# Stick-breaking attention with queries on the partitions: a reversed scan and transposes in place of products with ones

## The chip, the cores and the metric

The kernel runs on one core of a Trainium2 chip. The metric is the device time of one execution in microseconds (us), and the median over the runs is what counts.

## The reference

Three blocks follow one another on 512 tokens of width 2048, all in float32. The first block has an RWKV-7 recurrence, a pooling mixer and a stick-breaking attention; the second has chunked attention beside a state-space model (S5); the third has a forgetting attention. The change lies in the stick-breaking attention (12 heads of 64). Cut to what matters:

```
for q0 in range(0, S, 128):
    z = q[q0:q0+128] @ k[:q0+128].T
    causal = key < query
    log_1m = where(causal, log_sigmoid(-z), 0)
    after = reversed_cumsum(log_1m, over keys) - log_1m
    w = where(causal, exp(log_sigmoid(z) + after), 0)
    out = w @ v[:q0+128]
```

So each weight needs the sum of `log_1m` over all later keys of its row.

## The kernel before

Dense projections dominate. `dense` (line 286) yields after each of 16 k-steps of a unit; a step is three float32r matmuls of 512 columns (lines 310 to 312: high and low halves of weights and activations). Weights come by DMA in tiles of four steps and are split by `split_w` into a high part (`wh`, made by ScalarE, or by GpSimd where `POOL_SPLITS` says so) and a low part (`wl`, always VectorE). The splits run up to three tiles, some twelve steps, ahead of the matmuls that use them.

The order of every compute engine's instructions is the order of the program text. `stick` (line 1766) works on six pairs of heads, j = 0 to 5. While it handles pair j it calls `pump(n)`, which takes n steps out of a stream: the projections of pair j+1 (64 steps), or for the last pair two pooling groups and the first part of the output projection (87 steps). What `pump` has not taken is run at the end of the pair by a bare loop over the stream. The numbers of steps stand in `STICK_STEPS`; here they add up to 57 in each pair. `pump` also advances a side job, `extra`, once for every 1/`EXTRA_RATE` steps, which is every second step in `stick`; the bare loop does not. The side job is `s5_params` (line 899): 58 advances of small VectorE arithmetic for the S5 layer, and then eight tables, each of 14 advances on GpSimd and one DMA pair (lines 1004 to 1019). Whatever is left of it is emitted by `finish(self.extra)` after `stick`, ahead of the output projection `out_proj`. There, `s5_prep` computes with GpSimd and VectorE in turns, beginning in the third unit.

One pair before the change, with keys on the partitions (E and N are 128 x 1280 tiles holding four triangular key blocks):

- for each of the two heads: `scores` into three PSUM banks named `sm`; ScalarE takes Abs, Exp, Ln; pumped steps; VectorE makes E (log-sigmoid of z) and N (its counterpart, line 1811) and masks N; ScalarE and VectorE split N into `sbh` and `sbo`; in the first head the products with the values of the previous pair (`values`, line 1777) come next; pumped steps
- for each head: 20 matmuls of `sbh` and `sbo` with a triangle and with ones (line 1832) into three `sm` banks; VectorE subtracts them from E; ScalarE takes Exp; pumped steps; VectorE masks E; pumped steps.

There are four `sm` banks in all. A bank comes free when its last reader is done.

Of the kernel before, what the change touches and what calls it, by code (L numbers as in the profile page):

```python
# [9 lines left out]
F32 = mybir.dt.float32  # L10
F32R = mybir.dt.float32r
# [3 lines left out]
OP = mybir.AluOpType  # L15
# [15 lines left out]
STICK_WAIT = (8,6)  # L31
HEAD_LAG = (3,5,7)
RWKV_STEPS = (0,0,0,(13,6),4,4,3,3,3,1,1)
STICK_STEPS = ((7,7),(9,7),(4,8),(4,11))
EVEN_STEPS = ((3,8),(6,8),10)
ODD_STEPS = ((4,20),16)
LAST_STEPS = ((4,16),14)
# [103 lines left out]
class Kern:  # L141
# [49 lines left out]
    def constants(self, tmp):  # L191
        nc, c = self.nc, self.const
        jp = tmp.tile([128, 128], I32, name="jp")
        nc.gpsimd.iota(jp, pattern=[[1, 128]], base=0, channel_multiplier=-1)
        mk = lambda name: c.tile([128, 128], F32, name=name)
        self.ident = mk("ident")
        nc.vector.tensor_scalar(self.ident, jp, 0.0, None, op0=OP.is_equal)

        self.m16 = c.tile([128, 2], F32, name="m16")
        nc.vector.tensor_reduce(self.m16, self.ident.rearrange("p (a e i) -> p e a i", e=2, i=16),  # L200
                                op=OP.add, axis=mybir.AxisListType.XY)

        self.id2 = c.tile([128, 64], F32, name="id2")
        self.add(self.id2, self.ident[:, 0:64], self.ident[:, 64:128])

        self.m_lt = mk("m_lt")
        nc.vector.tensor_scalar(self.m_lt, jp, 0.0, None, op0=OP.is_gt)

        self.mk2 = c.tile([128, 2, 64], F32, name="mk2")
        for h in (0, 1):  # L210
            r = slice(64 * h, 64 * h + 64)
            nc.vector.tensor_scalar(self.mk2[r, 0], jp[r, r], 0.0, None, op0=OP.is_ge)
            nc.vector.tensor_scalar(self.mk2[r, 1], jp[r, r], 0.0, -1.0 if h == 0 else 1.0, op0=OP.is_gt, op1=OP.mult)

        blk = tmp.tile([128, 128], F32, name="blk")
        nc.vector.memset(blk, 0.0)
        for h in (0, 1):
            nc.vector.memset(blk[64 * h:64 * h + 64, 64 * h:64 * h + 64], 1.0)
        mr = lambda name: c.tile([128, 128], F32R, name=name)
        self.blk_r = mr("blk_r")  # L220
        self.copy(self.blk_r, blk)
        self.cen_r = mr("cen_r")
        V = nc.vector
        V.scalar_tensor_tensor(self.cen_r, blk, -1.0 / 64, self.ident, op0=OP.mult, op1=OP.add)
        self.heads = c.tile([128, 2], F32, name="heads")
        V.tensor_copy(self.heads, blk[:, 0:128:64])
        self.ident_r = mr("ident_r")
        self.copy(self.ident_r, self.ident)
        self.one = c.tile([128, 1], F32, name="one")
        nc.vector.memset(self.one, 1.0)  # L230
        self.ones_r = mr("ones_r")
        self.copy(self.ones_r, self.one.to_broadcast([128, 128]))

        self.suf_r = c.tile([128, 128], F32R, name="suf_r")
        nc.vector.tensor_scalar(self.suf_r, jp, 0.0, None, op0=OP.is_lt)

        self.omu = c.tile([128, 25], F32, name="omu")
        o, w = _PV["mu_a"]
        nc.vector.tensor_scalar(self.omu, self.pvt[:, o:o + w], -1.0, 1.0, op0=OP.mult, op1=OP.add)
        o, w = _PV["k_a"]  # L240
        self.oka = c.tile([128, 6], F32, name="oka")
        nc.vector.tensor_scalar(self.oka, self.pvt[:, o:o + w], -0.5, 1.0, op0=OP.mult, op1=OP.add)
        self.half = {}
        for n in ("k_a", "a0", "w0", "b_glu_2"):
            o, w = _PV[n]
            self.half[n] = c.tile([128, w], F32, name="half_" + n)
            nc.vector.tensor_scalar(self.half[n], self.pvt[:, o:o + w], 0.5, None, op0=OP.mult)
        self.qg8 = c.tile([128, 1], F32, name="qg8")
        nc.vector.tensor_scalar(self.qg8, self.pv("qn_g"), 0.125, None, op0=OP.mult)

        self.ipos = c.tile([128, 16], F32, name="ipos")
        nc.gpsimd.iota(self.ipos, pattern=[[1, 16]], base=1, channel_multiplier=0,
                       allow_small_or_imprecise_dtypes=True)
        nc.vector.reciprocal(self.ipos, self.ipos)

        self.reset = c.tile([128, 8, 64], BF16, name="reset")
        nc.vector.memset(self.reset, 1.0)
        nc.vector.memset(self.reset[:, :, 0:1], 0.0)
# [1500 lines left out]

    def causal(self, t):  # L1760

        d = t.rearrange("p (b n) -> p b n", n=256)[:, 0::2, 0:128]
        self.mul(d, d, self.m_lt[:, None, :].to_broadcast([128, 3, 128]))
        self.mul(t[:, 896:1024], t[:, 896:1024], self.m_lt)

    def stick(self, pool, tm, yd, acts, rs, yl):
        nc = self.nc
# [14 lines left out]

        last = None
        self.second_parts(pool)
        for j in range(6):
            pools = self.pools(6 + j, pool, tm, yd, acts, rs)
            self.stream = chain(self.stick_front(tm, j + 1, acts, rs, pool), *pools) if j < 5 else chain(
                *pools, self.out_ahead("w_out", *self.out_operands(yl, yd)))
            q, k, vt, gate = self.ready.pop(j)
            if j == 0:  # L1790
                q, k = self.stacked_q(pool, q), self.stacked_k(pool, k)
                self.pump(FIRST_STEPS)
            sums = []
            self.where = 2 if j else 1
            for p in (0, 1):
                z = [self.small() for _ in range(3)]
                at = lambda b: (z[OFF[b] // 512], OFF[b] % 512)
                for b in (0, 1, 3, 2):
                    t, o = at(b)
                    self.scores(t[:, o:o + 512 - 128 * b], p, slice(128 * b, 512), slice(128 * b, 128 * b + 128), q, k,  # L1800
                                True)
                N = L = pool.tile([128, 1280], F32, name="sbl", bufs=1)
                E = pool.tile([128, 1280], F32, name="sbe", bufs=3)
                for (o, n), t in zip(BANK, z):
                    self.act(L[:, o:o + n], t[:, 0:n], AF.Abs)
                self.act(L, L, AF.Exp, scale=-1.0)
                self.act(L, L, AF.Ln, bias=1.0)
                self.pump(STICK_STEPS[p][0])
                for (o, n), t in zip(BANK, z):
                    V.scalar_tensor_tensor(E[:, o:o + n], t[:, 0:n], 0.0, L[:, o:o + n], op0=OP.min, op1=OP.subtract)  # L1810
                    V.scalar_tensor_tensor(N[:, o:o + n], t[:, 0:n], 0.0, L[:, o:o + n], op0=OP.max,
                                           op1=OP.add)
                self.causal(N)
                hi = pool.tile([128, 1280], F32R, name="sbh", bufs=2)
                lo = pool.tile([128, 1280], F32R, name="sbo", bufs=2)
                self.split(hi, lo, N)
                sums.append((E, hi, lo))
                if last and p == 0:
                    values(*last)
                self.pump(STICK_STEPS[p][1])  # L1820
            for p, (E, hi, lo) in enumerate(sums):
                s = [self.small() for _ in range(3)]
                for b in (0, 1, 3, 2):
                    t, o = s[OFF[b] // 512], OFF[b] % 512
                    mm = []
                    for b2 in range(b, 4):
                        n = 512 - 128 * b2
                        for x in (hi, lo):
                            mm.append((t[:, o + 128 * (b2 - b):o + 128 * (b2 - b) + n],
                                       self.suf_r if b2 == b else self.ones_r, x[:, OFF[b2]:OFF[b2] + n]))  # L1830
                    for i, (o_, l_, r_) in enumerate(mm):
                        nc.tensor.matmul(o_, l_, r_, start=(i == 0), stop=(i == len(mm) - 1))
                for (o, n), t in zip(BANK, s):
                    self.sub(E[:, o:o + n], E[:, o:o + n], t[:, 0:n])
                self.act(E, E, AF.Exp)
                self.pump(STICK_STEPS[2 + p][0])
                self.causal(E)
                self.pump(STICK_STEPS[2 + p][1])
            last = j, vt, [E for E, _, _ in sums], gate
            self.where = 3  # L1840
            if j == 5:
                self.where = 0
                values(*last)
                self.out_last(gate, "w_out")
            for _ in self.stream:
                pass
# [74 lines left out]
```

## Time and profile before

| what | value |
|---|---|
| median of three runs | 3025.04 us (3021.55 to 3025.7) |
| profiled execution, time / span | 3014.29 us / 3012.5 us |
| TensorE matmul busy | 2935.8 us, 97% of the span |
| VectorE, ScalarE, GpSimd busy | 54%, 38%, 17% |
| mean granted TensorE clock | 0.987 of full speed |
| stick-breaking stage | about 598 us to 943 us of the span |

PE is TensorE, DVE is VectorE, ACT is ScalarE, POOL is GpSimd. Times in the views are us from the start of the span.

### The profile page before, as it was taken

What the parts mean: (1) busy time and instruction counts of PE and PEld (TensorE: products, weight loads), DVE (VectorE), ACT (ScalarE), POOL (GpSimd) and SP (SyncE); (2) the same over time, 40 slices, a digit from 0 to 9 for tenths busy, and PEclk for the clock granted to TensorE, in tenths of its full rate; (3) what the DMA queues carried; (4) which work ended last, traced back from release to release, by engine and by line L of the source; (5) the groups of instructions that cost most, each with busy time, mean ns of one, the idle gap of its engine ahead of it and who ended that gap; (6) DMA issues with size and microseconds to landing.
All of it is one profiled execution on the core that took longest, in us unless ns stands there. A gap on an engine that the chain in (4) does not pass through costs nothing. (4 is left out here: it accounts for less than half of the span.)

```text
span 3012.5 us, 42942 instructions
## 1 busy us (share of the span) xinstructions
PE 2935.8 (97%) x16068; PEld 2400.4 (80%) x16068; DVE 1618.0 (54%) x3140; ACT 1134.9 (38%) x2043; POOL 498.8 (17%) x951
## 2 busy tenths in 40 slices
PE   7999999999999999999999999999999999999998
PEld 5777777878887777788888887878888888888887
DVE  7555555477667665655554456344444444444533
ACT  4444443354454223222344454233333232323432
POOL 4111111014764220211100000111101010100011
PEclk9999999999999999999999999999999999999999
DMA  4212122322235556455433325443333333323443
GB/s 141 64 59 60 55 60 69 95 75 84 90 95 167 155 163 196 133 158 157 138 105 103 104 85 177 147 130 109 101 105 96 98 96 97 95 92 95 147 122 119
DMA packets 195298, 334.03 MB, mean 111 GB/s; under 512 B 29696, under 2 KB 44672, under 8 KB 193936
## 3 DMA queue, kind: packets, MB, share of 16 engines
q1 hardware_dynamic: 193808, 327.08, 35.9%
q0 software_dynamic: 1280, 4.20, 0.4%
q8 instruction: 126, 2.06, 0.3%
q14 instruction: 84, 0.69, 0.1%
HBM read 289.55 MB, written 42.70 MB: 110 GB/s over the span
## 5 line engine op out<-in xcount | busy, mean ns | idle before, releaser
L310 PE MATMUL big<-hi,wh 128*128 128x512 f32 x3440 | 1375.7, 400 | 4.1 <-ACT hi L180 2.9
L312 PE MATMUL big<-hi,wl 128*128 128x512 f32 x3440 | 1350.9, 393 | 7.3 <-DVE wl L162 6.8
L311 PE MATMUL big<-lo,wh 128*128 128x512 f32 x3440 | 1349.1, 392 | 2.3 <-DVE lo L162 2.3
L162 DVE TENSOR_TENSOR wl<-wr,wh 128x512 fp32r<-128x512 f32 x884 | 648.3, 745 | 721.0 <-ACT wh L180 711.7
L312 PEld LDWEIGHTS big<-hi,wl 128*128 128x128 f32 x3440 | 649.6, 189 | 153.5 <-DVE wl L162 15.8
L310 PEld LDWEIGHTS big<-hi,wh 128*128 128x128 f32 x3440 | 649.7, 189 | 150.0 <-issue 10.7
L311 PEld LDWEIGHTS big<-lo,wh 128*128 128x128 f32 x3440 | 650.1, 189 | 133.2 <-DVE lo L162 5.6
L180 ACT ACTIVATE wh<-wr 128x512 fp32r<-128x512 f32 x820 | 505.8, 626 | 632.0 <-PE big L311 515.7
L1231 POOL TENSOR_SCALAR dm<-cb,cq 128x128 f32<-128x128 f32 (+1 forms) x64 | 42.4, 663 | 598.1 <-DVE mx L674 580.1
L680 ACT ACTIVATE pm<-pm,mx 128x128 f32<-128x128 f32 (+3 forms) x128 | 70.5, 552 | 178.1 <-DVE mx L676 178.1
L162 POOL TENSOR_TENSOR ssq<-ssq,sq 128x512 f32<-128x512 f32 (+1 forms) x43 | 54.6, 1269 | 380.1 <-ACT sq L175 359.5
L162 DVE TENSOR_TENSOR tm<-big,rs 128x512 f32<-128x512 f32 x86 | 59.2, 688 | 73.4 <-PE big L312 73.3
L175 ACT ACTIVATE sq<-xn 128x512 f32<-128x512 f32 (+1 forms) x47 | 28.8, 613 | 177.8 <-DVE xn L162 166.3
L279 POOL CAST wh<-wr 128x512 fp32r<-128x512 f32 x64 | 47.7, 747 | 143.5 <-PE big L311 93.0
L180 ACT ACTIVATE pt<-sm 128x512 f32<-128x512 f32 (+3 forms) x96 | 43.4, 526 | 62.7 <-PE sm L708 62.7
L162 DVE TENSOR_TENSOR xn<-big,xr 128x512 f32<-128x512 f32 (+1 forms) x50 | 33.3, 667 | 56.7 <-PE big L312 45.5
L1610 POOL MEMSET xi<- 64x16 f32 x6 | 0.7, 119 | 371.4 <-DVE xi L1609 371.4
L180 ACT ACTIVATE qk<-tm 128x512 fp32r<-128x512 f32 x32 | 20.2, 633 | 96.2 <-DVE tm L1366 48.1
L162 POOL TENSOR_TENSOR ssq<-xn 128x512 f32<-128x512 f32 x3 | 3.1, 1040 | 310.4 <-DMA wr<-w_out_even 143.5
L162 DVE TENSOR_TENSOR pl<-sm,pt 128x512 fp32r<-128x512 f32 (+1 forms) x48 | 25.9, 596 | 44.3 <-ACT pt L180 44.3
L686 DVE TENSOR_SCALAR pm<-pm,sm 128x128 f32<-128x128 f32 (+3 forms) x128 | 43.3, 400 | 1.1
L1366 DVE SCALAR_TENSOR_TENSOR tm<-big,rs 128x512 f32<-128x512 f32 x34 | 23.4, 689 | 36.9 <-PE big L312 36.9
(445 smaller groups left out, 3140.4 us busy)
## 6 DMA issues: line engine op xcount, KB each, us to landing
wr<-w_in_odd SPq DMA_DIRECT2D x256, 256.0 KB, 3.3
wr<-w_in SPq DMA_DIRECT2D x228, 256.0 KB, 3.1
wr<-w_in_even SPq DMA_DIRECT2D x192, 256.0 KB, 3.5
wr<-w_out SPq DMA_DIRECT2D x64, 256.0 KB, 3.8
wr<-w_out_even SPq DMA_DIRECT2D x64, 256.0 KB, 3.4
wr<-w_out_odd SPq DMA_DIRECT2D x64, 256.0 KB, 3.3
xr<-x SPq DMA_DIRECT2D x48, 256.0 KB, 3.0
yl<-y SPq DMA_DIRECT2D x45, 256.0 KB, 3.8
```

The costliest lines, as they stand in the source:

```text
L162: (eng or self.nc.vector).tensor_tensor(out, a, b, op=op)
L175: self.nc.scalar.activation(out, x, f, scale=scale)
L180: self.nc.scalar.activation(out, x, AF.Copy, scale=scale)
L279: self.nc.gpsimd.tensor_copy(wh, wr)
L310: nc.tensor.matmul(ps, wh[:, i], hi, start=(k == 0), stop=False)
L311: nc.tensor.matmul(ps, wh[:, i], lo, start=False, stop=False)
L312: nc.tensor.matmul(ps, wl[:, i], hi, start=False, stop=(k == n - 1))
L680: nc.scalar.activation(d, d, AF.Exp, bias=mx[:, b:b + 1], accum_out=sm[:, b:b + 1])
L686: V.tensor_scalar(d, d, sm[:, b:b + 1], None, op0=OP.mult)
L1231: nc.gpsimd.tensor_scalar(D[:, QOFF[b]:QOFF[b] + n], cb[:, 0:n], -1.0, cq[:, b, h:h + 1], op0=OP.mult, op1=OP.add)
L1366: self.nc.vector.scalar_tensor_tensor(t, ps, scale, rs, op0=OP.mult, op1=OP.mult)
L1610: G.memset(X.rearrange("p i c -> p (i c)")[:, 0:256:17], 1.0)
```

## The change

Queries go on the partitions and keys along the free axis, in the layout that `qblocks` and `turn` already use in the second block. The 20 matmuls with triangle and ones and the split of N go. In their place one `tensor_tensor_scan` per head runs backwards over the 1280 columns (`rows` holds a 0 where a block of keys begins anew), and one subtraction in SBUF takes the sums, shifted by a column, from E. The finished weights are turned by `keys(p)`, that is `turn`: ten float32 transposes into three `sm` banks and three ScalarE copies to SBUF, since `values` needs the keys on the partitions. The order within a pair changes: the scan, subtraction and Exp of the first head now come ahead of the second head's scores; the first head is masked and turned inside the second head's part, the second one at the end. `STICK_STEPS` changes with it and adds up to 37 in each pair. `EXTRA_RATE` stays.

```
-STICK_STEPS = ((7,7),(9,7),(4,8),(4,11))
+STICK_STEPS = ((7,0,5,3),(6,2,4,7),3)
...
-        self.ones_r = mr("ones_r")
-        self.copy(self.ones_r, self.one.to_broadcast([128, 128]))
...
+        self.m_gt = mk("m_gt")
+        nc.vector.tensor_scalar(self.m_gt, jp, 0.0, None, op0=OP.is_lt)
...
     def causal(self, t):
-        d = t.rearrange("p (b n) -> p b n", n=256)[:, 0::2, 0:128]
-        self.mul(d, d, self.m_lt[:, None, :].to_broadcast([128, 3, 128]))
-        self.mul(t[:, 896:1024], t[:, 896:1024], self.m_lt)
+        m = self.m_gt[:, None, :].to_broadcast([128, 2, 128])
+        d = t[:, 384:640].rearrange("p (b n) -> p b n", n=128)
+        self.mul(d, d, m)
+        d = t[:, 768:1280].rearrange("p (b n) -> p b n", n=256)[:, :, 128:256]
+        self.mul(d, d, m)
...
+        self.rows = pool.tile([128, 1280], BF16, name="rows", bufs=1)
+        V.memset(self.rows, 1.0)
+        for b in range(4):
+            o = 1279 - (QOFF[b] + 128 * b + 127)
+            V.memset(self.rows[:, o:o + 1], 0.0)
...
+            def keys(p):
+                W.append(pool.tile([128, 1280], F32, name="sbw", bufs=3))
+                self.turn(Es[p], W[p])
...
             for p in (0, 1):
-                z = [self.small() for _ in range(3)]
...
+                z = self.qblocks()
+                for b in (3, 0, 2, 1):
+                    t, o, n = z[b]
+                    self.scores(t[:, o:o + n], p, slice(128 * b, 128 * b + 128), slice(0, n), q, k, False)
+                z = [z[3][0], z[0][0], z[1][0]]
...
                 self.pump(STICK_STEPS[p][0])
+                if p:
+                    self.causal(Es[0])
                 for (o, n), t in zip(BANK, z):
                     V.scalar_tensor_tensor(E[:, o:o + n], t[:, 0:n], 0.0, L[:, o:o + n], op0=OP.min, op1=OP.subtract)
                     V.scalar_tensor_tensor(N[:, o:o + n], t[:, 0:n], 0.0, L[:, o:o + n], op0=OP.max,
                                            op1=OP.add)
                 self.causal(N)
-                hi = pool.tile([128, 1280], F32R, name="sbh", bufs=2)
-                lo = pool.tile([128, 1280], F32R, name="sbo", bufs=2)
-                self.split(hi, lo, N)
-                sums.append((E, hi, lo))
-                if last and p == 0:
+                if p:
+                    self.pump(STICK_STEPS[p][1])
+                    keys(0)
+                elif last:
                     values(*last)
-                self.pump(STICK_STEPS[p][1])
-            for p, (E, hi, lo) in enumerate(sums):
-                s = [self.small() for _ in range(3)]
...
-                        nc.tensor.matmul(o_, l_, r_, start=(i == 0), stop=(i == len(mm) - 1))
-                for (o, n), t in zip(BANK, s):
-                    self.sub(E[:, o:o + n], E[:, o:o + n], t[:, 0:n])
+                self.pump(STICK_STEPS[p][2])
+                V.tensor_tensor_scan(N[:, ::-1], self.rows, N[:, ::-1], 0.0, OP.mult, OP.add)
+                self.sub(E[:, 0:1279], E[:, 0:1279], N[:, 1:1280])
                 self.act(E, E, AF.Exp)
-                self.pump(STICK_STEPS[2 + p][0])
-                self.causal(E)
-                self.pump(STICK_STEPS[2 + p][1])
-            last = j, vt, [E for E, _, _ in sums], gate
+                Es.append(E)
+                self.pump(STICK_STEPS[p][3])
+            self.causal(Es[1])
+            self.pump(STICK_STEPS[2])
+            keys(1)
+            last = j, vt, W, gate
```

## Rows read from the trace of the kernel before

**Rows 1.** The page: busy time, share of the span and instructions of each engine

```profile
PE 2935.8 (97%) x16068; PEld 2400.4 (80%) x16068; DVE 1618.0 (54%) x3140; ACT 1134.9 (38%) x2043; POOL 498.8 (17%) x951
```

**Rows 2.** Waits of PE, 590 to 960 us: who waited for whom, total, times, longest

```profile
PE pa L1753 <- DVE tm L162: 2.9, 3, 1.2
PE pa L382 <- ACT tm L175: 2.4, 2, 1.8
PE sm L1832 <- DVE sbl L1811: 0.8, 2, 0.7
```

**Rows 3.** Timeline of PE, third pair: start, duration, engine, line, operation

```profile
715.12 0.40 PE L310 MATMUL big<-hi,wh 128*128 128x512 f32 x1
...
720.00 2.37 PE L1777 MATMUL sm<-sbe,BK 128*64 128x512 f32 x16
...
727.21 0.39 PE L749 MATMUL sm<-q,k 128*128 128x512 f32 x1
...
738.71 0.39 PE L310 MATMUL big<-hi,wh 128*128 128x512 f32 x1
...
739.39 0.40 PE L1832 MATMUL sm<-sbh,suf_r 128*128 128x512 f32 x1
...
742.10 0.44 PE L310 MATMUL big<-hi,wh 128*128 128x512 f32 x1
```

**Rows 4.** Timeline of ACT, third pair

```profile
715.32 1.34 ACT L175 ACTIVATE sbl<-sm 128x512 f32<-128x512 f32 x3
...
719.27 1.27 ACT L177 ACTIVATE sbl<-sbl 128x1280 f32<-128x1280 f32 x1
...
729.30 1.36 ACT L175 ACTIVATE sbl<-sm 128x512 f32<-128x512 f32 x3 [1.26 <-DVE sbo L162]
...
736.27 0.62 ACT L180 ACTIVATE wh<-wr 128x512 fp32r<-128x512 f32 x1
```

**Rows 5.** Timeline of DVE, third pair

```profile
721.10 0.69 DVE L162 TENSOR_TENSOR wl<-wr,wh 128x512 fp32r<-128x512 f32 x1 [4.28 <-ACT wh L180]
721.71 0.68 DVE L1810 SCALAR_TENSOR_TENSOR sbe<-sm,sbl 128x512 f32<-128x512 f32 x1
...
725.26 0.89 DVE L162 TENSOR_TENSOR sbl<-sbl,m_lt 128x384 f32<-128x384 f32 x2
727.55 1.66 DVE L162 TENSOR_TENSOR sbo<-sbl,sbh 128x1280 fp32r<-128x1280 f32 x1 [1.40 <-ACT sbh L180]
729.13 0.68 DVE L162 TENSOR_TENSOR RKV<-sm,RKV 128x512 f32<-128x512 f32 x1
```

**Rows 6.** Line 1402, the scans of 512 columns: duration ns min/median/max

```profile
L1402 DVE TENSOR_TENSOR_SCAN tm<-reset,tm x6: 1224/1224/1225, 63.3 to 424.3; 128x512 f32<-128x512 bf16 x6
```

**Rows 7.** Timeline of PE in the second block: ten transposes and the next matmul

```profile
1539.46 1.25 PE L708 MATMUL sm<-ident,pm 128*128 128x128 f32 x10
1540.46 0.48 PE L310 MATMUL big<-hi,wh 128*128 128x512 f32 x1
```

**Rows 8.** Timeline of PE, first pair: after the wait for squares, 21 dense matmuls

```profile
629.34 1.05 PE L382 MATMUL pa<-heads,tm 128*128 128x2 f32 x8 [1.80 <-ACT tm L175]
630.26 0.48 PE L310 MATMUL big<-hi,wh 128*128 128x512 f32 x1
...
636.87 1.09 PE L405 MATMUL pa<-ident,tm 128*128 128x128 f32 x8
```

**Rows 9.** Stretches of 2 us there: busy by engine, then granted clock

```profile
632.00:634.00 2.00, 2.00 (x6) 1.52 (x6) 1.79 (x10) 1.84 (x2) 0.61 (x1) 0.50 0.42 121
```

**Rows 10.** Timeline of POOL: one table, the last table, then the output projection

```profile
857.20 0.11 POOL L1008 MEMSET fi<- 128x4 f32 x1 [1.07 <-DMA s5w<-fi]
...
858.26 0.61 POOL L279 CAST wh<-wr 128x512 fp32r<-128x512 f32 x1
...
878.71 0.54 POOL L1019 DMA_DIRECT2D s5w<-fi  x1
...
937.67 0.54 POOL L1019 DMA_DIRECT2D s5w<-fi  x1
975.76 1.04 POOL L162 TENSOR_TENSOR ssq<-xn 128x512 f32<-128x512 f32 x1 [37.55 <-DVE xn L162]
...
982.94 0.40 POOL L162 TENSOR_TENSOR s5y<-pr,s5b 128x128 f32<-128x128 f32 x1
```

**Rows 11.** Timeline of DVE at the start of the output projection

```profile
983.79 1.22 DVE L162 TENSOR_TENSOR s5z<-s5y 64x128 f32<-64x128 f32 x3 [0.21 <-POOL s5y L162]
```

**Rows 12.** Timeline of PE, after the last pair's products with the values

```profile
943.38 0.50 PE L310 MATMUL big<-hi,wh 128*128 128x512 f32 x1
```

More of the change, by code (lines that the diff above doesn't have):

```diff
@@ L230, in constants @@
         nc.vector.memset(self.one, 1.0)
-        self.ones_r = mr("ones_r")
-        self.copy(self.ones_r, self.one.to_broadcast([128, 128]))
-        self.suf_r = c.tile([128, 128], F32R, name="suf_r")
-        nc.vector.tensor_scalar(self.suf_r, jp, 0.0, None, op0=OP.is_lt)
+        self.m_gt = mk("m_gt")
+        nc.vector.tensor_scalar(self.m_gt, jp, 0.0, None, op0=OP.is_lt)
         self.omu = c.tile([128, 25], F32, name="omu")
@@ L1792, in stick @@
                 self.pump(FIRST_STEPS)
-            sums = []
             self.where = 2 if j else 1
+            Es, W = [], []
+            def keys(p):
+                W.append(pool.tile([128, 1280], F32, name="sbw", bufs=3))
+                self.turn(Es[p], W[p])
             for p in (0, 1):
-                z = [self.small() for _ in range(3)]
[L1797 to L1803, printed above, removed]
+                z = self.qblocks()
[3 more added lines that the diff above has]
+                z = [z[3][0], z[0][0], z[1][0]]
+                N = L = pool.tile([128, 1280], F32, name="sbl", bufs=2)
+                E = pool.tile([128, 1280], F32, name="sbe", bufs=2)
                 for (o, n), t in zip(BANK, z):
@@ L1813, in stick @@
                 self.causal(N)
-                hi = pool.tile([128, 1280], F32R, name="sbh", bufs=2)
-                lo = pool.tile([128, 1280], F32R, name="sbo", bufs=2)
-                self.split(hi, lo, N)
-                sums.append((E, hi, lo))
-                if last and p == 0:
-                    values(*last)
-                self.pump(STICK_STEPS[p][1])
-            for p, (E, hi, lo) in enumerate(sums):
-                s = [self.small() for _ in range(3)]
[L1823 to L1831, printed above, removed]
-                        nc.tensor.matmul(o_, l_, r_, start=(i == 0), stop=(i == len(mm) - 1))
-                for (o, n), t in zip(BANK, s):
-                    self.sub(E[:, o:o + n], E[:, o:o + n], t[:, 0:n])
-                self.act(E, E, AF.Exp)
-                self.pump(STICK_STEPS[2 + p][0])
-                self.causal(E)
-                self.pump(STICK_STEPS[2 + p][1])
-            last = j, vt, [E for E, _, _ in sums], gate
+                if p:
+                    self.pump(STICK_STEPS[p][1])
+                    keys(0)
+                elif last:
+                    values(*last)
+                self.pump(STICK_STEPS[p][2])
+                V.tensor_tensor_scan(N[:, ::-1], self.rows, N[:, ::-1], 0.0, OP.mult, OP.add)
+                self.sub(E[:, 0:1279], E[:, 0:1279], N[:, 1:1280])
+                self.act(E, E, AF.Exp)
+                Es.append(E)
[4 more added lines that the diff above has]
+            last = j, vt, W, gate
             self.where = 3
```

## The prediction

> **What bounds the kernel now.** I read the page first: PE is busy for 97% of the span, every other engine for little more than half or less [rows 1]. So a matmul that goes is time gained, and a wait of PE is time lost, one for one. Then PE's waits in the stage: in some 350 us it hardly waits, and the sums with ones wait 0.8 us in all, for a VectorE instruction that reads the score banks [rows 2]. That names the resource to watch: of the four `sm` banks three hold the second head's scores, and the next user needs three. Then the timelines of one undisturbed pair, the third, on PE, ACT and DVE [rows 3 to 5]. The reader is to see two clocks running: PE's own work from the first head's scores to the next use of the banks, and the chain of ACT and DVE that frees them. In the old order they are matched: PE takes 739.39 - 715.12 = 24.3 us and finds the banks just free.
>
> **What goes and comes on PE.** The 20 matmuls of a head take 742.10 - 739.39 = 2.71 us [rows 3]; ten transposes take 1540.46 - 1539.46 = 1.00 us [rows 7]. Scores and value products keep their columns. Twelve heads times 1.71 us: **-20.5 us**. The row for the transposes is of the same helper with the same tiles, so I put only 1 us either way on this.
>
> **The first head's turn, inside the second head.** PE's cover between the end of the first scores and `keys(0)` is now 7 + 5 + 3 steps, `values`, the second scores, and 6 + 2 steps. A step is 739.39 - 738.71 = 0.68 us, `values` 2.3 us, scores 1.27 us [rows 3]: 23 x 0.68 + 3.6 = 19.2 us, where the old order had 30 steps and 24.3 us. The second and third transposed banks can't be written before the second head's score banks are read.
>
> Now the chain, from 715.12 as zero. Abs, Exp, table load and Ln end at +5.4 (719.27 + 1.27) [rows 4]; a weight split on ACT and its low part on DVE stand next in the queues, E and N begin at +6.6 and the mask of N ends at +11.0 (725.26 + 0.89) [rows 5]. So far nothing changes. Before, the split of N took the time up to 729.2 and the second Abs began at +14.2. Now DVE does the gate product of `values` (0.6, from 729.13 to the next issue), one or two low parts of weights (0.8 for 1.25 tiles in five steps), the scan, the subtraction and then ACT the Exp of E, all ahead of the second Abs, since ACT keeps the order of the text. The scan of 512 takes 1.22 us [rows 6]; in proportion 1280 take 3.06, and 2.8 if 0.15 us of the row is fixed, as I take it; a scan at the rate of the 1280-column subtraction (1.66 us) [rows 5] is the lower bound, and 4.2 (half as much again for running backwards, which no row shows) the upper. Subtraction 1.5, hand-off 0.1, Exp 1.3. Sum: 11.0 + 0.6 + 0.8 + 2.8 + 1.5 + 0.1 + 1.3 = +18.1. The second head's Abs, Exp, load and Ln take 1.36 + 3 x 1.28 = 5.2: +23.3. The stream's squaring and a weight split on ACT (736.27 + 0.62 is 1.05 after the Ln's end), its low part on DVE and the mask of E, which stand ahead of the second E and N in the queue, add 1.1 + 0.6 + 0.8: +25.8. Two banks of E and N take 2.6: **+28.4**. PE arrives at +19.2 and can do two transposes: it waits about 9.1 us. With everything foreign left out of the chain (0.6, 0.8, the first split 1.1, and the 2.5) it is 23.4 and the wait 4 us, the lower bound; 10.5 us the upper one. The first pair has no `values` (2.3 us less cover), but GpSimd does its splits, so no ACT split stands in the chain: 7.6 us. Sum: 5 x 9.1 + 7.6 = **+53 us** (24 to 63). PE's queue is held as a whole meanwhile; behind it stand the projections, for which nobody else waits.
>
> **The clock after such a wait.** In the first pair PE waited 1.8 us around tiny matmuls; the granted clock fell to 0.50 [rows 9], the 1.2 GHz level, and the 21 dense matmuls up to the next transposes took 636.87 - 630.26 = 6.6 us, where seven steps are 4.8 [rows 8]. 1.8 us lost, six times: **+11 us** (0 to 12).
>
> The Trainium skill (TensorE: Matmul & The Clock Gate, "Part 4: PE-mode transpose") says that transposes do not count as work that brings the clock up. In the trace ten transposes at the full clock are followed by dense matmuls at the usual pace [rows 7], but none stands behind a long wait. By the page the ten behind each wait would run at half speed without helping: an estimate of 1 us more each, 6 us in all; the sum does without it.
>
> **The second head's turn.** From the release at +28.4 PE does 4 + 7 + 3 steps and the first turn, 10.5 us. DVE and ACT need the last bank and mask (1.7), a low part (0.6), scan 2.8, subtraction 1.5, Exp 1.4, a split and low part (1.2), mask 0.8: 10.0 us. About even: I put 0.5 us for each pair. In the last pair `values` follows the copies of the turn at once, some 2 us. **+5 us** (0 to 9). The other pairs' copies lie under the 27 steps that the bare loop runs.
>
> **The side job.** This is the part that the diff does not show. It needs 171 advances. Old: 8 first steps at 0.4, then 6 x 57 at 0.5: 174, and the last table leaves at 937.67 [rows 10], before the stage ends. New: 3 + 6 x 37 / 2 = 114. Left are 56, which is four of the eight tables, and `finish` puts them into POOL's queue in one piece. A table takes 878.71 + 0.54 - 857.20 = 22.0 us, less five casts of 0.61: 19.0 [rows 10]; with 2.5 us of waiting for its DMAs four take 83 us. POOL then owes the sums of squares, the clearing of four tiles and the first product of `s5_prep`, 7.2 us (975.76 to 982.94 [rows 10]): 90 us after the last pumped step. DVE wants that product at 983.8 [rows 11], 40.4 us after the value products [rows 12]. Now 20 more steps (13.6) and the turn, its copies and `values` (1.0 + 2.2 + 2.3) come between: 60 us after the last pumped step. DVE is late by 30, and behind that instruction in its queue stand the low parts of the weights, for which PE waits. Splits run some 13 steps ahead; DVE already trails PE by some 3 us here, so about 7 us are covered. I take 22 us of PE idle and 2 for the clock: **+24 us** (0 if POOL gets through its tables in 60 us, 33 if nothing covers).
>
> **What disappears.** The waits for squares and values in the stage (5.3 us [rows 2]) meet an emptier ACT and DVE in the bare loop; I take half: **-3 us** (0 to -9, with the clock behind them). Constants and the `rows` tile are a few VectorE instructions beside dense work and cost nothing; without that cover they would be 3 us.
>
> **Sum.** -20.5 + 53 + 11 + 5 + 24 - 3 = **+69.5 us** on the profiled execution, whose 3014.29 us (span 3012.5 and 1.8 around it) lie 10.75 us under the median. The difference carries over: 3025.0 + 69.5 = **3094 us**.
>
> **Rivals.** *The tables are hidden.* POOL gets through its products faster once the stage's VectorE work is over, and the splits ahead cover the rest. For it: the pair of instructions is the only place where VectorE needs POOL, and the cover of 7 us is worked out from the order of the text. Against it: 90 against 60 us leaves little room. Then +45 us: 3070 us.
>
> *The chain fits under the cover* (the other side). The place is `keys(0)`; its price is the 53 + 11 us above. It decides where the chain is shorter than 19.2 + 20.5 / 6 = 22.6 us: below that the stage gains. For it: ACT and DVE are idle half the time [rows 1]. Against it: the bare chain with nothing foreign in it is 23.4 us already. With no wait at all the stage gives -20.5 + 5 - 3, which is 3006 us with the tables hidden and 3030 us with their price.
>
> *PE finds the waits longer than summed*, because a scan running backwards takes 4.2 us in both heads and the second turn waits too: six times 1.4 + 2.8 more, 3120 us. Nothing in the trace speaks for a slower backward walk, nor against it.
>
> **Chances.** Both waits, as summed: 0.58. Tables hidden: 0.25. Chain fits: 0.08 (faster in 0.05, unchanged in 0.03). Longer waits: 0.09. About 0.2% (6 us) is what a measurement of this kernel can tell from no change; beyond it: faster 0.05, same 0.04, slower 0.91. The range goes from a bank wait near its lower half with hidden tables, 3048, to the summed case with the upper bounds of the waits, 3115.
>
> **What would show it.** In PE's waits: six for the second head's E and N at line 708, of 7 to 10 us each, and a granted clock of 0.5 behind them. In POOL's timeline: four tables in one piece between the last cast and the first sum of squares, and DVE waiting for POOL at the first S5 product with PE waiting for `wl` behind it. In DVE's groups: twelve scans near 2.8 us. PE's busy time in the stage should fall by some 20 us. Wrong would be: no wait at line 708 above 3 us, or scans at 1.4 us; then the chain fits and the kernel is not slower.

## The result, and the profile after

The changed kernel takes 3107.36 us (median of 4, 3101.55 to 3114.01), the kernel before 3025.37: a ratio of 1.0278, with a 95% interval of 1.0255 to 1.0301. It is slower by 82 us; 3094 had been forecast. Line numbers after are smaller by two: the dense products stand in L308 to L310, the turns in L706, the scores in L747, E and N in L1823 and L1824, the scan in L1834.

The page of the kernel after, busy time and share of each engine [rows 1]:

```profile
PE 2944.4 (95%) x15948; PEld 2404.0 (77%) x15948; DVE 1627.2 (52%) x3121; ACT 1145.6 (37%) x2081; POOL 496.9 (16%) x936
```

PE is busy for no less than before; what grew is its idle time, from 3012.5 - 2935.8 = 76.7 us to 3105.8 - 2944.4 = 161.4, with the spans of the two profiled executions. The waits of PE from 590 to 1110 us say where [rows 2]:

```profile
PE big L308 <- DVE xn L162: 40.4, 1, 40.4
PE sm L706 <- DVE sbe L162: 31.5, 13, 7.6
PE sm L706 <- DVE sbl L1824: 19.9, 12, 3.4
```

There are two losses: 51.4 us at the turns (the transposes of `keys`), in every pair, and one wait of 40.4 us behind the stage. First the turns. PE in the third pair [rows 3]:

```profile
728.96 0.39 PE L308 MATMUL big<-hi,wh 128*128 128x512 f32 x1
...
747.80 0.39 PE L308 MATMUL big<-hi,wh 128*128 128x512 f32 x1
...
751.09 0.41 PE L706 MATMUL sm<-ident,sbe 128*128 128x128 f32 x2 [2.44 <-DVE sbe L162]
754.50 0.90 PE L706 MATMUL sm<-ident,sbe 128*128 128x128 f32 x3 [3.00 <-DVE sbl L1824]
755.91 1.30 PE L706 MATMUL sm<-ident,sbe 128*128 128x128 f32 x5 [0.51 <-DVE sbl L1824]
756.87 0.77 PE L308 MATMUL big<-hi,wh 128*128 128x512 f32 x1
...
759.14 0.39 PE L308 MATMUL big<-hi,wh 128*128 128x512 f32 x1
```

From the end of the first scores, 728.96, PE's cover (the products that it has to do meanwhile) lasts to 747.80 + 0.68 = 748.5, which is +19.5 (forecast: +19.2). It then waits for the mask of the first head's E, and after two transposes for the score banks. The chain behind this, first on ACT, then on DVE [rows 4, 5]:

```profile
746.08 1.27 ACT L175 ACTIVATE sbe<-sbe 128x1280 f32<-128x1280 f32 x1 [9.86 <-DVE sbe L162]
...
747.77 1.34 ACT L175 ACTIVATE sbl<-sm 128x512 f32<-128x512 f32 x3
...
751.73 1.27 ACT L177 ACTIVATE sbl<-sbl 128x1280 f32<-128x1280 f32 x1
```

```profile
741.47 2.82 DVE L1834 TENSOR_TENSOR_SCAN sbl<-rows,sbl 128x1280 f32<-128x1280 bf16 x1
744.33 1.71 DVE L162 TENSOR_TENSOR sbe<-sbe,sbl 128x1279 f32<-128x1279 f32 x1
...
750.53 0.75 DVE L162 TENSOR_TENSOR sbe<-sbe,m_gt 128x256 f32<-128x256 f32 x2
753.03 0.69 DVE L1823 SCALAR_TENSOR_TENSOR sbe<-sm,sbl 128x512 f32<-128x512 f32 x1 [1.75 <-ACT sbl L177]
```

ACT stands idle for 9.86 us until the subtraction behind the scan is done, because the Exp of E comes next in its queue; only then may it read the second head's scores. E and N end at 756.55 (756.13 + 0.42), +27.6 against a forecast of +28.4.

Behind the wait the clock is down [rows 9]. A stretch of 2 us of the kernel after (its length, busy time of PE, PEld, DVE, ACT and POOL, then granted clock, DMA share, GB/s):

```profile
756.00:758.00 2.00, 2.00 (x8) 1.80 (x9) 1.97 (x8) 1.35 (x3) 0.00 (x0) 0.50 0.00 0
```

0.50 is the 1.2 GHz level; two steps take 759.14 - 756.87 = 2.27 us in place of 1.36.

Now the wait behind the stage. The queue of SP, then SP's waits from 940 to 1080 us:

```profile
1010.32 0.33 SPq L440 DMA_DIRECT2D yl<-y  x1
1062.42 0.33 SPq L628 DMA_DIRECT2D xr<-x  x1
```

```profile
SPq L628 <- DMA s5w<-fr: 34.5, 2, 17.2
SPq L628 <- DMA s5w<-fi: 17.0, 3, 15.5
```

The first load of `out_proj` is that of `xr`. SP does not issue it before the tables `fr` and `fi` have left for memory, and for 52 us nothing behind it in the queue goes out either. GpSimd builds the left-over tables in one piece [rows 10] (the first clearing for the first of four tables, and the last table's DMA):

```profile
976.16 0.10 POOL L1005 MEMSET fr<- 128x4 f32 x1 [1.28 <-DMA s5w<-fr]
...
1059.75 0.54 POOL L1017 DMA_DIRECT2D s5w<-fi  x1
```

DVE waits for `xr`, and PE, for 40.4 us, for the PSUM bank that DVE's addition frees [rows 11, 12]:

```profile
1065.11 0.69 DVE L162 TENSOR_TENSOR xn<-big,xr 128x512 f32<-128x512 f32 x1 [41.23 <-DMA xr<-x]
```

**The account.** The stage from its first scores to the dense products behind the last values, kernel before, then after (span, then busy PE, PEld, DVE, ACT, POOL):

```profile
598.70:943.40 344.70, 337.88 (x1683) 277.63 (x1681) 249.90 (x532) 168.94 (x221) 180.69 (x417) 0.99 0.30 90
```

```profile
604.60:975.83 371.23, 319.40 (x1503) 255.07 (x1501) 249.94 (x496) 174.76 (x248) 112.59 (x218) 0.93 0.23 75
```

The stage is 26.5 us longer, though in its last pair 20 steps (13.6 us) now come behind it: 40.1 us. From there to the first `xn` it is 1065.11 - 975.83 = 89.3 us; before, 974.9 - 943.4 = 31.5 us. Of the 57.8 us between them 13.6 are those steps, and 44.2 remain. These two are 84.3 of the 93.3 us between the two profiled executions. The rest is 5.9 us ahead of the stage, where the code is the same, and 3.1 us after the first `xn`.

The group of these additions in the kernel before, shortest, median and longest duration in ns, first and last start:

```profile
L162 DVE TENSOR_TENSOR xn<-big,xr x16: 673/684/692, 974.9 to 1172.7; 128x512 f32<-128x512 f32 x16
```

### The profile page after: what moved, and what is told of

Read it like the earlier page. It is cut to its first block, busy times and chain, and to the rows that moved or that the text cites. A ratio compares the mean times of both kernels' runs of the same rounds, so it can differ in the third digit from the quotient of the medians.

```text
span 3105.8 us, 42707 instructions
## 1 busy us (share of the span) xinstructions
PE 2944.4 (95%) x15948; PEld 2404.0 (77%) x15948; DVE 1627.2 (52%) x3121; ACT 1145.6 (37%) x2081; POOL 496.9 (16%) x936
## 3 DMA queue, kind: packets, MB, share of 16 engines
q0 software_dynamic: 1280, 4.20, 0.4%
## 5 line engine op out<-in xcount | busy, mean ns | idle before, releaser
L308 PE MATMUL big<-hi,wh 128*128 128x512 f32 x3440 | 1384.9, 403 | 44.5 <-DVE xn L162 41.4
L310 PE MATMUL big<-hi,wl 128*128 128x512 f32 x3440 | 1355.9, 394 | 4.0 <-DVE wl L162 3.7
L308 PEld LDWEIGHTS big<-hi,wh 128*128 128x128 f32 x3440 | 654.5, 190 | 191.9 <-DVE xn L162 42.7
L310 PEld LDWEIGHTS big<-hi,wl 128*128 128x128 f32 x3440 | 653.6, 190 | 147.5 <-DVE wl L162 8.1
L180 ACT ACTIVATE wh<-wr 128x512 fp32r<-128x512 f32 x835 | 515.3, 626 | 664.7 <-PE big L309 539.7
L277 POOL CAST wh<-wr 128x512 fp32r<-128x512 f32 x49 | 39.3, 805 | 259.5 <-PE big L309 152.9
L706 PE MATMUL sm<-ident,sbe 128*128 128x128 f32 x120 | 25.5, 355 | 51.4 <-DVE sbe L162 31.5
L706 PEld LDWEIGHTS sm<-ident,sbe 128*128 128x128 f32 x120 | 17.1, 179 | 60.9 <-issue 24.0
```

Of the source, the lines that this page charges most:

```text
L180: self.nc.scalar.activation(out, x, AF.Copy, scale=scale)
L277: self.nc.gpsimd.tensor_copy(wh, wr)
L308: nc.tensor.matmul(ps, wh[:, i], hi, start=(k == 0), stop=False)
L310: nc.tensor.matmul(ps, wl[:, i], hi, start=False, stop=(k == n - 1))
L706: nc.tensor.transpose(ps[o // 512][:, o % 512:o % 512 + 128], Pm[:, QOFF[b] + 128 * kb:QOFF[b] + 128 * kb + 128], self.ident)
```

## The experiments

Each is the changed kernel with the edit shown, except where the old one is named; the kernel before took 3020.5 to 3023.8 us (medians) beside them.

**The side job packed into the stage.**

```
-EXTRA_RATE = (.4,.5,.5,.5)
+EXTRA_RATE = (.4,.775,.775,.775)
```

> The changed kernel with one number different: the side job that prepares the S5 tables is advanced at every 1.3rd pumped step and not at every second, so that its 171 advances fit into 37 steps per pair. Theory: the two losses are separate, and the 40.4 us wait in front of the output projection exists only because four tables are left over. Then that wait goes (below 5 us), the 51 us of waits at the turns of the first head stay within 45 to 60, and the time is 3107 less 44, about 3063 (3055 to 3070). Rival 1: the tail belongs to the new order itself (turn, copies and values at the end of the last pair); then the wait stays near 40 and the time near 3105. Rival 2: more VectorE work of the side job in each pair lengthens the chain that frees the score banks; then the waits at the turns grow by 10 us or more, above 62, and the time is above 3073.

Measured: 3102.82 us (ratio to before 1.0265, 1.0241 to 1.0289). The 40 us wait is gone, but the time stays. Rival 2 is right in what it says of the turns and the time, by far more than it named, but not in its reason: what is late is a cast on GpSimd. PE's waits of this run, and one turn of the second head, on POOL, DVE and PE:

```profile
PE sm L706 <- DVE sbe L162: 72.3, 12, 9.0
PE sm L706 <- DVE sbl L1824: 11.7, 12, 2.6
```

```profile
916.94 2.80 POOL L162 TENSOR_TENSOR pb<-fr,qi 128x64 f32<-128x64 f32 x1
...
932.21 0.61 POOL L277 CAST wh<-wr 128x512 fp32r<-128x512 f32 x1
```

```profile
932.85 0.69 DVE L162 TENSOR_TENSOR wl<-wr,wh 128x512 fp32r<-128x512 f32 x1 [8.48 <-POOL wh L277]
933.46 0.75 DVE L162 TENSOR_TENSOR sbe<-sbe,m_gt 128x256 f32<-128x256 f32 x2
```

```profile
934.02 2.37 PE L706 MATMUL sm<-ident,sbe 128*128 128x128 f32 x10 [8.82 <-DVE sbe L162]
```

A cast of weights stands behind table products in GpSimd's queue, a low part behind the cast on DVE, the mask behind the low part, and PE behind the mask. The turns now wait 84 us, and DVE waits 44.4 us in all for such casts. The tables cost nearly what they did, in another place.

**More cover, tables still left over.**

```
-STICK_STEPS = ((7,0,5,3),(6,2,4,7),3)      EXTRA_RATE .5
+STICK_STEPS = ((7,0,5,3),(6,15,4,7),6)     EXTRA_RATE .35
```

> The changed kernel with 13 more steps of other products ahead of the first head's turn and 3 more ahead of the second's (53 pumped steps per pair in place of 37), and the side job slowed to every 2.9th step so that it still has its 114 advances and four tables left over. Theory: the waits at the turns are a lack of cover, 6.4 to 9 us at the first head and 1 to 2.5 us at the second, and 13 steps are 8.8 us, 3 are 2.0. Then the waits at the turns fall from 51 to below 12 us, the granted clock stays up behind them, and with the tail of about 44 us unchanged the time is 3107 - 51 - 8 + 6 = 3054 (3044 to 3062). Rival: the weight splits and squares that come with the steps stand in the same ACT and DVE queues ahead of the second head's E and N and lengthen the chain as much as the cover; then half the wait stays, 25 us, and the time is about 3080.

Measured: 3086.57 us (1.0217, 1.0196 to 1.0239); neither number. The waits at the turns fall to 1.4 us, so they were a lack of cover. But of these 50 us only 20.8 are gained; the rest goes elsewhere. PE's waits from 500 to 1120 us, and one of the new ones, on PE and DVE:

```profile
PE big L308 <- DVE xn L162: 53.3, 1, 53.3
PE big L310 <- DVE wl L162: 19.7, 9, 3.9
```

```profile
751.80 0.50 PE L310 MATMUL big<-hi,wl 128*128 128x512 f32 x1 [2.47 <-DVE wl L162]
```

```profile
746.95 0.69 DVE L1823 SCALAR_TENSOR_TENSOR sbe<-sm,sbl 128x512 f32<-128x512 f32 x1 [1.55 <-ACT sbl L177]
...
751.06 0.69 DVE L162 TENSOR_TENSOR wl<-wr,wh 128x512 fp32r<-128x512 f32 x1
```

The dense products that give the cover need low parts, and these stand on DVE behind an E that waits for the Ln. And the wait behind the stage grows by 13 us: 16 steps more are pumped, so that 16 fewer (10.9 us) stand between the last values and the addition that needs `xr`, while GpSimd ends its tables 82 us after the last values, much as before (85 us).

**Both.** 53 steps as above, side job at 0.54.

> Both edits: 53 pumped steps per pair as in the run with more cover, and the side job advanced at 0.54 per step, so that its 171 advances are done within the stage. Theory: the losses are separate and add up, so what is left of the change is its gain on PE (20.5 us less, of which the transposes behind no wait take 1.0 us per head): waits at the turns below 12 us, wait before the output projection below 5 us, 3107 - 53 - 44 = 3010 (3002 to 3016), faster than before by 0.3 to 0.8%. Rival 1: they overlap (a PE that runs faster in the stage meets the tables later): 3020 to 3035. Rival 2: the score banks wait whatever the cover: about 3035.

Measured: 3046.67 us (1.0080, 1.0058 to 1.0102), above the theory and above both rivals. Waits at the turns: 0.5 us; none behind the stage; PE waits 21.5 us for low parts, and DVE 18.9 us for GpSimd's casts within the stage. Of the 82 us 25 remain, so most of the loss was the number of steps and the side job, but the gain on PE doesn't come through. The stage of this run says where it stays:

```profile
607.50:970.30 362.80, 330.42 (x1550) 261.78 (x1548) 270.20 (x511) 168.60 (x245) 208.80 (x416) 0.95 0.26 87
```

PE is idle in it for 362.80 - 330.42 = 32.4 us, against 6.8 in the kernel before. Its work is only 4.7 us less, with the 4 steps (2.7 us) that come behind this stage added: from start to start and without waits the transposes take 13 us where the sums took 34, but the dense products take 10 us more than before, at a granted clock of 0.95 on average against 0.99.

**The old kernel with four tables left over** (before: `EXTRA_RATE` .5 to .325).

> The kernel before the change with one number different: the side job is advanced at 0.325 per pumped step and not at 0.5, so that it ends the stage with 114 advances, four tables left over, as in the changed kernel. Theory: the tail is a matter of the side job alone and nothing of the turn, the scan or the transposes. The old order then shows the same wait of PE before the output projection, longer by the 20 steps (13.6 us) that its pumped steps reach further into the last pair: 50 to 58 us, and 3025 + 52 to 60 = 3077 to 3085. Rival: the tail comes from the new order at the end of the last pair; then the old code with four tables left over stays at 3025 to 3035.

Measured: 3074.42 us (1.0177, 1.0156 to 1.0197), 52.5 us above the kernel before beside it, where 52 to 60 were expected. The old code shows the same wait of PE:

```profile
PE big L310 <- DVE xn L162: 57.8, 1, 57.8
```

The price of the left-over tables is thus shown without any part of the new computation.

**Why the wait is where it is.** Three runs put the left-over tables into buffers of a pool that stays open: first `fr`, `fi` and the scratch products, in a free RKV buffer; then also copies of the factors `qr`, `qi`, made by VectorE; then these copies made by GpSimd.

```
+late = self.fr.tile([128, 8, 3, 64], F32, name="RKV") if self.where == 0 else None
+(second run) V.tensor_copy(x, y)        # qr, qi into a BK buffer
+(third run)  nc.gpsimd.tensor_copy(x, y)
```

> The changed kernel; only the tables that are left over after the stage are built in tiles of a pool that stays open (a free RKV buffer holds fr, fi and the two scratch products), not in the stage's own pool, whose space the output projection takes over. Work and order are the same. Theory: the 40.4 us wait is one of space: the load of xr, first in SP's queue, may not be issued before the tables that lie in its space have left, and everything behind it in the queue stands. Then the load goes out some 50 us earlier, the wait of PE before the second column group of the output projection goes, and what is left is the wait that was predicted, VectorE for GpSimd's first S5 product with the low parts of the weights behind it, 15 to 25 us: 3107 - 44 + 15 to 25 = 3078 to 3090. Rival 1: the load is late because of the queue's or the DMA engines' own state; then nothing changes, 3100 to 3110. Rival 2: VectorE's need of GpSimd costs nothing either (splits run ahead far enough); then 3060 to 3068.

Measured: 3103.31 us (1.0271, 1.0249 to 1.0294), the time that rival 1 gives. SP's wait is still there, with another name: `xr` now waits for a GpSimd product.

```profile
SPq L628 <- POOL RKV L162: 49.3, 1, 49.3
```

That this product is one that reads `qr` from the closed pool was only argued here; so the next run.

> As the run with the left-over tables in an open pool, and now the twelve small factors qr and qi that every table reads are copied out of the stage's pool too (twelve VectorE copies of 32 columns). In that earlier run SP still stood 49.3 us, but for a GpSimd product on RKV and no longer for the DMAs of fr and fi. Theory: it was still space; the last reader of something in the closed pool was a GpSimd product that read qr. With nothing of the tables left in the closed pool the load of xr goes out before 1010, the 40 us wait of PE goes, and what is left is VectorE's wait for GpSimd's first S5 product, 15 to 25 us: 3078 to 3090. Rival 1: the load waits for GpSimd's queue whatever the space; then SP stands 45 us or more again and the time is 3100 to 3110. Rival 2: VectorE's need of GpSimd is covered; 3060 to 3068.

Measured: 3124.13 us (1.0340, 1.0318 to 1.0363). SP stands no more at L628, but VectorE came to the twelve copies only at 1021.9, so the tables began 45 us late; PE waited 53.2 us at another place. So the third:

> As the run before with nothing of the tables left in the closed pool, but the twelve factors are copied by GpSimd and not by VectorE, whose in-order queue came to the copies only at 1021.9 and so held the tables back by some 45 us. The tables can now begin at 976 as in the changed kernel. Theory: VectorE's wait for GpSimd's first S5 product is a second wait behind the one of the load. VectorE asks for it near 1037; four tables of 16.3 us from 978, the sums of squares, the clearing and the product (7 us) end at 1050; the wait is then about 13 us and PE loses 8 to 14: 3107 - 44 + 8 to 14 = 3071 to 3077. By the value summed in the prediction (22 us and 2 for the clock) it is 3087. Rival 1: the splits that run ahead cover it, and PE loses under 3 us: 3063 to 3066. Rival 2: the load of xr is held again by GpSimd: 3100 or more.

Measured: 3107.07 us (1.0285, 1.0257 to 1.0314). SP's queue, then PE and DVE of this run:

```profile
1012.48 0.33 SPq L440 DMA_DIRECT2D yl<-y  x1
1013.17 0.33 SPq L628 DMA_DIRECT2D xr<-x  x1
```

```profile
1077.86 0.80 PE L310 MATMUL big<-hi,wl 128*128 128x512 f32 x1 [35.95 <-DVE wl L162]
```

```profile
1071.23 0.38 DVE L162 TENSOR_TENSOR s5z<-s5y 64x128 f32<-64x128 f32 x1 [38.73 <-POOL s5z L1048]
1074.63 1.20 DVE L162 TENSOR_TENSOR s5z<-s5y 64x128 f32<-64x128 f32 x3 [3.02 <-POOL s5y L162]
```

The load goes out at once: the wait for `xr` was one of space. In its place stands a wait where one was forecast. At the first S5 products VectorE waits for GpSimd, 38.73 us for the clearing of their tile `s5z` (L1048) and 3.02 us more for GpSimd's product, and PE waits behind it for `wl`: 36 us. So the time is the same, where 3071 to 3077 had been expected. Both waits hang on one event, the end of the tables; the earlier had hidden the later.

**No scan in the first head.**

```
-V.tensor_tensor_scan(N[:, ::-1], self.rows, N[:, ::-1], 0.0, OP.mult, OP.add)
+if p:  (the same scan)
```

> The changed kernel without the scan of the first head of each pair (six of the twelve scans; the subtraction then takes N itself). Theory: the whole scan of 2.9 us stands in the chain that frees the score banks. Then the waits at the first head's turn fall by 2.9 us in each pair, the sum at the turns from 51 to about 34 us, and the time from 3107 to 3088 (3084 to 3093), the clock included. Rival 1: the chain is held by something beside the scan (weight splits that wait for ACT or GpSimd, the table loads); the waits fall by less than 6 us in all and the time stays above 3100. Rival 2: GpSimd, whose products stand still while a scan runs, gains as well: the tail gets shorter by up to 6 times 2.9 us, and the time falls below 3080.

Measured: 3092.46 us (1.0234, 1.0207 to 1.0261): 14.9 less than the change, and in the range expected. The waits at the turns fall from 51.4 to 32.9 us:

```profile
PE sm L706 <- DVE sbl L1824: 18.2, 12, 2.9
PE sm L706 <- DVE sbe L162: 14.7, 6, 4.6
```

Of these 18.5 us 16.3 are at the first head's turns, where six scans of 2.9 us (17.4) were left out: the scan stands in the chain with nearly its full length.

**Other orders.** Low parts ahead of E and N, `STICK_STEPS = ((7,0,5,3),(14,10,4,7),6)`, side job .51; then the same with `POOL_SPLITS = {1:1,4:1}`.

> As the run with both edits, but the steps that cover the chain are pumped ahead of the second head's E and N (14 before, 10 between them and the turn; there 6 before, 15 between), the side job at 0.51 per step. PE's order around the turn is nearly the same; what changes is VectorE's: the low parts of the weights stand ahead of E and N and not behind them. Theory: what took the place of the bank waits in that run, 19 us of PE waiting for low parts in front of the turn, comes from VectorE's in-order queue, where the low parts stand behind an E that waits for the Ln. Then that wait falls below 6 us and the time from 3047 to 3022 to 3030. Rival: the low parts now delay E and N by 2 to 3 us, the bank wait comes back by as much, and the time stays at 3040 to 3050.

> As the run with the reordered steps, and GpSimd makes none of the weights' high parts in pairs two to six (half of them before, in the pumped steps); ACT makes them. Theory: GpSimd's table products and its weight casts are in one queue, and VectorE waits some 19 us in all for casts that stand behind table products; without them VectorE's waits for GpSimd go, and the time is 5 to 15 us below that of the run with the reordered steps: 3010 to 3022. Rival: ACT, which is in the chain that frees the banks, gets some four more splits of 0.6 us per pair ahead of the second head's Abs and Ln; the waits move to the turns, and the time is 5 to 15 us above that run.

Measured: 3070.65 (1.0163, 1.0138 to 1.0188) and 3070.63 us (1.0164, 1.0141 to 1.0188). Both theories fall, and so do the times of both rivals. In the first PE's wait for low parts falls from 21.5 to 7.7 us, and the first head's turns wait for the score banks for 1.7 us in all, so the bank wait does not come back. PE waits elsewhere instead: at the transposes of v (L1751), and at L706 now at the second head's turns:

```profile
PE pa L1751 <- DVE tm L162: 18.6, 5, 6.5
PE sm L706 <- DVE sbe L162: 13.7, 3, 5.9
PE sm L706 <- ACT wh L180: 8.1, 3, 2.7
```

In the second DVE's waits for casts are gone, and PE waits 12.0 us for ACT's high parts instead; the time is the same.

**The Exp of E behind the second head's Ln**, alone, and with 47 steps and the side job at .61.

```
 if p:
-    self.causal(Es[0])          # ahead of E and N; now behind them
+    self.act(Es[0], Es[0], AF.Exp)
```

> The changed kernel with one step moved: the Exp of the first head's E stands on ACT behind the second head's Abs, Exp and Ln and not ahead of them, and the mask of E behind the second head's E and N on VectorE. Steps and side job as in the changed kernel. Theory: what makes the chain long is ACT's order: Abs waits for the scan and the subtraction only because the Exp of E stands ahead of it (9.9 us idle on ACT in the third pair). With the move the second head's scores are read some 4 us earlier, at the price of a table load (1.3 us) behind the Ln: the waits at the turns fall from 51 to about 25 to 30 us, the time from 3107 to 3075 to 3083. Rival: the mask of E, now last, ends as late as E and N did (Exp, load and mask are 3.3 us); the waits fall by less than 8 us and the time stays above 3095.

> The same move, 7 more steps ahead of the first head's turn and 3 more ahead of the second's (47 in all), and the side job at 0.61 per step so that nothing of it is left over. Theory: with the chain 4 us shorter 7 steps (4.8 us) cover it, the low parts of the weights no longer stand behind an E that waits for the Ln, and the gain of the change on PE shows: waits at the turns below 10 us, no wait before the output projection, 3010 to 3025 beside a kernel before of about 3021. Rival: the tables, denser by a fifth, hold the weight casts on GpSimd, and with them VectorE's queue; PE then waits 20 to 30 us for low parts and masks, and the time is 3040 to 3055.

Measured: 3108.89 (1.0280, 1.0251 to 1.0309) and 3059.66 us (1.0128, 1.0104 to 1.0152). The move alone does nothing, as its rival says: the banks come free earlier, and the mask of E, now last, holds the turn; the waits at the turns are 47.5 us. With ten more steps and the side job packed in they are 48.0 us, but the first head's turns have only 7.5 of it; 40.4 are at the second head's, and DVE waits 30.3 us for casts. That is the rival's mechanism, with more than its 20 to 30 us and a time above its range.

No version here beats the old order. Whether weight splits further ahead would give back the last 25 us of the run with both edits was not tried.

## Why the prediction was right, and where its sizes were off

**The direction and the two places.** Slower was forecast for two reasons, a wait at the first head's turn and four tables left over, and both are there. The chain was summed to +28.4 and ended at +27.6 in the third pair, PE's cover +19.2 and was +19.5. The six waits at the first head's turns are 5.3 to 9.0 us each, in two or three pieces, where 7 to 10 were to be the sign. The scan, put at 2.8 us from a 512-column row, takes 2.82 us as a rule and 2.90 on average.

**The stage**, all terms: 45.5 us forecast, 40.1 measured. Errors in it balance, which is luck. Waits were forecast as 53 + 5 - 3 = 55 us; PE's idle time in the stage grew by (371.23 - 319.40) - (344.70 - 337.88) = 45.0 us. The first head's turns wait some 39 us, not 53, since PE does its transposes in pieces as the mask and the banks come; the second head's wait 12 and not 5; and the old waits of the stage go almost altogether, -6 and not -3. PE's work was forecast as -20.5 + 11 = -9.5 us; it is 319.40 + 13.6 - 337.88 = -4.9 (the fall of PE's busy time by some 20 us that was to be the sign is there, 18.5, but 13.6 of it are the steps that moved). The products that were exchanged give 12 us and not 20.5, the dense products take 7 us more, where 11 were forecast for the clock (both counted in PE's timeline from start to start, without waits). The 12 come from the transposes:

```profile
L706 PE MATMUL sm<-ident,sbe 128*128 128x128 f32 x120 | 25.5, 355 | 51.4 <-DVE sbe L162 31.5 <-DVE sbl L1824 19.9
```

Their busy time is 25.5 us. Counted like [rows 7], to the start of the next product and without the waits between, ten take 1.8 us on average and not 1.0; at the first head's turn of the third pair 756.87 - 751.09 - 3.00 - 0.51 = 2.27 us. In the run with more cover, where the turns hardly wait, ten are mostly followed by the next product after 1.01 us. So the row was right for transposes behind dense work and wrong behind a wait: five take 756.87 - 755.91 = 0.96 us at the low clock. The sentence from the Trainium skill (TensorE: Matmul & The Clock Gate, "Part 4: PE-mode transpose"), that transposes do not count as work that brings the clock up, had been turned into an estimate of 1 us more for ten behind a wait. The trace agrees with that size at the first head's turns (2.27 against 1.01 us); it does not tell whether they failed to raise the clock or only ran before it rose, since the dense products after them are slow for two or three steps as well.

**The side job** is the term that was mis-sized: +24 forecast, 44.2 measured. That four tables would be left and that GpSimd would build them in one piece is right, and their length too: 1059.75 + 0.54 - 976.16 = 84 us, forecast 83. What was wrong is the first reader. The prediction followed DVE's need of GpSimd's product, and missed that the output projection's tiles lie in the space of the closed pool, so that SP's load of `xr` must wait for the tables; the addition that needs it stands 62 matmuls, some 14 us, earlier in PE's program. The forecast place is real, as the third of the runs with open buffers shows, but its price was off as well: 36 us, not 22. There GpSimd was late by 38.7 + 3.0 = 41.7 us and not 30: it was still at the table before and began the left-over ones 7.8 us after the last pumped step (twelve copies, 1.8 us, included), and they took 88.8 us. The splits that run ahead covered the other 5.8 us, near the 7 assumed.

**The rivals.** Hidden tables (3070): not so, and not to be had by packing them into the stage, where they hold the casts. That the S5 products are the only place where VectorE needs GpSimd, the reason given for this rival, does not hold in the stage: it needs the casts too. A chain that fits (3006 to 3030): not with these steps; with 53 steps it fits, and then 3047 is measured and not 3010, for the low parts become the next wait. Longer waits (3120), for a slower scan: no, as its duration shows; but the second head's turn does wait longer than summed.

**Against the medians.** The forecast added its sum to the median, since the old kernel's profiled execution lay 10.75 us under it. That holds: the 5.9 us ahead of the stage are a matter of that one execution, for the old kernel with the slower side job reached its first scores at 604.41, the changed one at 604.60. So the 84.3 us of the account stand beside 82 on the medians. 3094 was too low by 13, and against the account by 15: the side job is +20 of it, the stage -5.

## What to carry to other kernels

When an edit changes how many steps a loop pumps, count what else is driven by these steps: here half the loss came from a side job that no line of the diff names, and the old kernel shows the same loss when only that is changed. A late engine has a price that is set by its first reader, and a load into space that it still uses is a reader; taking away one reader uncovers the next. Making the engine earlier helps only where the engines have room for its work: packed into the stage as it was, the side job cost the same at the turns (3102.82 us), and with more cover as well 25 us still remained. Cover is no free filler: the products that hide a chain on ACT and DVE need those engines themselves.

## What the runs showed of the hardware

A GpSimd product stands still while VectorE runs a long instruction with two inputs in SBUF. In the kernel after, GpSimd, then DVE:

```profile
959.70 2.81 POOL L162 TENSOR_TENSOR pb<-fi,qi 128x64 f32<-128x64 f32 x1
962.58 1.54 POOL L162 TENSOR_TENSOR fr<-pa,pb 128x64 f32<-128x64 f32 x1
964.20 0.29 POOL L162 TENSOR_TENSOR pa<-fi,qr 128x64 f32<-128x64 f32 x1
```

```profile
959.51 2.91 DVE L1834 TENSOR_TENSOR_SCAN sbl<-rows,sbl 128x1280 f32<-128x1280 bf16 x1
962.45 1.49 DVE L162 TENSOR_TENSOR sbe<-sbe,sbl 128x1279 f32<-128x1279 f32 x1
```

The product of 64 columns takes 2.81 us under the scan and the next 1.54 under the subtraction; the third, under neither, 0.29. The Trainium skill (SBUF — State Buffer, "Who interferes with whom") says that a VectorE instruction with two SBUF inputs contends with a GpSimd instruction that reads SBUF, and the trace agrees. So each head now has 2.8 + 1.5 = 4.3 us in which a GpSimd product gets nowhere, where the subtraction that the change removes took 1.7 [rows 5].

A scan of 1280 columns that walks backwards takes 2.82 us: 2.20 ns per column, where the forward one of 512 columns [rows 6] takes 2.39. Walking backwards costs nothing that shows.
